# The seventh product's result is copied out of PSUM by ScalarE before VectorE adds to it

## The chip, the cores and the metric

The program runs on one core of one Trainium2 chip. The metric is the device time of one execution in microseconds. A core has five engines that matter here, each with its own in-order queue of instructions: TensorE (PE in the profile: matrix products, into the on-chip accumulator memory PSUM), VectorE (DVE), ScalarE (ACT), GpSimd (POOL), and SyncE (SP), which issues most of the transfers between the chip's main memory and the on-chip memory SBUF. An instruction starts when its own engine has reached it and when the semaphores on which it waits have been raised by other engines. A late instruction delays all that stand behind it in its queue.

## The reference, cut to what matters

The model has two layers over 1024 latent tokens of width 1024. The change lies in the second (odd) layer, the multi-scale pooling mixer, in its input projection:

```python
z = h @ p["w_in"]                       # 1024 tokens x 1024  @  1024 x 4096
u, g = jnp.split(z, [W_POOL], axis=-1)  # values u and gates g, 2048 wide each
d = multiscale_pool(u.reshape(bn * rows, GRID_W, W_POOL))   # window means minus u, per 64-token row
y = jnp.einsum("bngi,gij->bngj", d, p["w_grp"]).reshape(bn, n, W_POOL) * p["scale"]
return (y * jax.nn.silu(g)) @ p["w_out"]
```

The kernel folds `w_grp` into the value half of `w_in` beforehand (the tiles `wfold`), so the values come out of one product and only have to be pooled, scaled and multiplied by silu of the gates.

## The kernel before, in words

Everything is laid out with channels on the 128 partitions and tokens along the free axis. The input `h` of the second layer is held as 8 channel tiles of 1024 tokens. The value product and the gate product of two output tiles (2 x 128 channels, 1024 tokens) make one **block**; there are eight blocks (`m` = 0, 2, ... 14), each with a value product and then a gate product.

Each of these products is done by a Strassen-like scheme in the function `quad`: the 2 x 2 arrangement of output quarters (two channel tiles `i`, two token halves `h`) is made from seven products in place of eight. Every one of the seven is 12 matmuls: 4 channel steps times 3, because fp32 accuracy is made from a high and a low part of both operands (high x high, high x low, low x high; lines L989, L991, L992). So a block is 2 x 7 x 12 = 168 matmuls of 128x128 by 512. The weights of the seven products are sums and differences made on VectorE and split into high and low parts (`wquad`; ACT casts the high part at L102, DVE subtracts to get the low part at L103); they are loaded two tiles at a time by SP into the buffers `wr_v` and `wr_g`.

The seven products of a `quad` accumulate in three PSUM banks, named `qa`, `qc` and `qb` in the profile, out of a ring of four. In the order of the program:

- product 1 into `qa`; ACT copies `qa` to `qb` (L1005), so that `qb` starts from product 1;
- product 5 into `qc`; ACT copies it to an SBUF tile as a kept part of quarter (1,1) (L1033, `s_v` or `s_g`);
- product 6 onto `qb`; ACT copies that as a kept part of quarter (0,1);
- product 2 onto `qa`: quarter (0,0) is complete and ACT takes it out;
- **product 7 onto `qb`** (operand `x_t3`): with the kept part of quarter (1,1) it makes that quarter. This is the place of the change;
- product 3 onto `qc` (operand `x_b22`): with the kept part of (0,1) it makes that quarter, taken out by VectorE's add;
- product 4 onto `qb` (operand `x_t4`): completes quarter (1,0).

Product 4 accumulates onto the same bank out of which the result of product 7 has to be read first, so PE's first matmul on `x_t4` waits until whoever reads `qb` after product 7 is done. Before the change that reader is VectorE, which adds the kept part straight out of PSUM: `vp<-qb_v,s_v` at L1470 for the values and `y<-qb_g,s_g` at L1481 for the gates. Only in the last gate product (`m == NK - 2`) ACT copies `qb` into the output tile first (L1479) and VectorE adds in SBUF.

The code emits instructions with priorities, the evacuations with a high one; a list scheduler that estimates durations then sets the order in each engine's queue. So PE's queue often holds the start of the next product between two products of this one, and the order of VectorE's queue mixes the adds with the pooling (L1372 to L1390), the weights' sums and splits, and the sums for the third matrix product (L913 to L916). A change in one instruction's engine can therefore move others.

Of the kernel before, what the change touches and what calls it, by code (L numbers as in the profile page):

```python
# [55 lines left out]
def body(ctx, tc, xT, ctxT, cc, ccol, modT, modW, win, gw, wout, wu, grp, wg, wo1, small, edge, ident, outT):  # L56
    nc = tc.nc
    mult, add, sub = ALU.mult, ALU.add, ALU.subtract
# [16 lines left out]
    def dtile(name, dt=F32):  # L75
        return dpool.tile([P, S], dt, tag="d", name=name)
# [69 lines left out]
    def col(o, n=1):  # L146
        return sm[:, o : o + n]
# [69 lines left out]
    def mod_tile(t, l, m, raw, vecs, junk):  # L217
        for i, vec in enumerate(vecs):
            nc.vector.scalar_tensor_tensor(out=junk, in0=raw, scalar=1.0, in1=vec,
                                           op0=mult, op1=mult, accum_out=t[:, i, m : m + 1])  # L220
        n = len(vecs)
        v = t[:, :n, m]
        nc.vector.tensor_tensor(out=v, in0=v, in1=col(O_MB + l * 3 * KT + m).to_broadcast([P, n]), op=add)
# [6 lines left out]
    def load_c(i, t, part=slice(0, D)):  # L230
        nc.sync.dma_start(t, cc[i, part].partition_broadcast(P))
        nc.scalar.activation(t, t, AF.Silu)
# [420 lines left out]
    with ExitStack() as actx:  # L653
# [88 lines left out]
        for j in range(KT):  # L742
# [27 lines left out]
            if state is None:  # L770
                for m in range(2 * KT, 3 * KT):
# [5 lines left out]
                    in1=col(O_MB + 2 * KT, KT), op=add)  # L777
# [173 lines left out]
    def wquad(src, name, ring, late=False):  # L951
        raw = []
        for i in range(2):
            r = wpool.tile([P, D], F32, tag="wr", name=f"wr_{name}_{i}")
            loaded[0] = nc.sync.dma_start(r, src[i])
            raw.append(r)
        a11, a12 = [raw[0][:, h] for h in HALF]
        a21, a22 = [raw[1][:, h] for h in HALF]

        def op(v, i):  # L960
            t = ring(f"wq_{name}_{i}")
            split(v, t[:, HALF[0]], t[:, HALF[1]], nc.vector)
            return t

        p1 = op(a11, 1)
        if late:
            p4 = op(a22, 4)
        s3 = ttile(f"ws_{name}")
        nc.vector.tensor_tensor(out=s3, in0=a11, in1=a21, op=sub)
        nc.vector.tensor_tensor(out=a21, in0=a21, in1=a22, op=add)  # L970
        nc.vector.tensor_tensor(out=a11, in0=a21, in1=a11, op=sub)
        if not late:
            p5 = op(a21, 5)
        p6 = op(a11, 6)
        p2 = op(a12, 2)
        p7 = op(s3, 7)
        nc.vector.tensor_tensor(out=a12, in0=a12, in1=a11, op=sub)
        if late:
            p5 = op(a21, 5)
        p3 = op(a12, 3)  # L980
        if not late:
            p4 = op(a22, 4)
        return p1, p2, p3, p4, p5, p6, p7
# [16 lines left out]
    def quad(w, name, ops, put, ahead=None):  # L1000
        p1, p2, p3, p4, p5, p6, p7 = w
        a, c, b = psum(f"qa_{name}"), psum(f"qc_{name}"), psum(f"qb_{name}")
        prod(a, p1, ops["b11"], True, False)
        with tc.high_priority(offset=EVAC):
            evac = nc.scalar.copy(b, a)  # L1005
        prod(c, p5, ops["t1"], True, False)
        with tc.high_priority(offset=EVAC):
            put(1, 1, c, 0)
        prod(b, p6, ops["t2"], False, False)
        with tc.high_priority(offset=EVAC):  # L1010
            put(0, 1, b, 0)
        prod(a, p2, ops["b21"], False, True)
        with tc.high_priority(offset=EVAC):
            put(0, 0, a, None)
        w = None
        if ahead is not None:
            with tc.issue_after(evac.ins):
                w = ahead()
        prod(b, p7, ops["t3"], False, False)
        with tc.high_priority(offset=EVAC):  # L1020
            put(1, 1, b, 1)
        prod(c, p3, ops["b22"], False, True)
        with tc.high_priority(offset=EVAC):
            put(0, 1, c, 1)
        prod(b, p4, ops["t4"], False, True)
        with tc.high_priority(offset=EVAC):
            put(1, 0, b, None)
        return w


    def keep_part(parts, name, i, x):
        parts[i] = ttile(f"s{i}_{name}")
        nc.scalar.copy(parts[i], x)  # L1033
# [275 lines left out]
    def v_weights(m, ring):  # L1309
        return wquad([wfold[(m + i) // 4][(m + i) % 4].rearrange("p k c -> p (k c)") for i in range(2)], f"v{m}", ring)  # L1310
# [42 lines left out]
    def rows(t):  # L1353
        return t.rearrange("p (r t) -> p r t", t=ROW)
# [37 lines left out]
    NK = 2 * KT  # L1392
# [12 lines left out]
    def y_keep(m):  # L1405
        b11, b12, b21, b22 = y_blocks(m)
        for name, v in (("b11", b11), ("b21", b21), ("b22", b22)):
            y_store(m, name, v)

    def y_sums(m):  # L1410
        t = block_sums(*y_blocks(m), vtile(f"yt3_{m}"), nc.vector)
        for name in ("t1", "t2", "t3", "t4"):
            y_store(m, name, t[name])
# [18 lines left out]
    def y_operands(part, raws, names=BOPS, alloc=None):  # L1432
        for name in names:
            y_operand(yops[part], part, name, next(raws),
                      alloc or (dtile if name in ("b11", "b21", "t4") else d2tile))
# [11 lines left out]
    def wo1_weights(part, m):  # L1447
        return wquad([wo1[m + i, part] for i in range(2)], f"wo{part}_{m}", wo1_ring,
                     part == 1 and m >= KT - 4)
# [3 lines left out]
    for m in range(0, NK, 2):  # L1453
        wv = wv0 if m == 0 else v_weights(m, ring_x)
        if m == 0:
            for i in range(4):
                vp = wpool.tile([P, D], F32, tag=("wh", "wl")[i % 2], name=f"vp{i}")[:, : NR * PW]
                vp = vp.rearrange("p (r t) -> p r t", t=PW)
                nc.gpsimd.memset(vp[:, :, 0:PADW], 0.0)
                nc.gpsimd.memset(vp[:, :, PADW + ROW : PW], 0.0)  # L1460
                vps.append(vp)
        parts = {}

        def to_tokens(i, h, x, part):
            if part is None:
                nc.scalar.copy(token[i][h], rows(x))
            elif part == 0:
                keep_part(parts, f"v{m}", i, x)
            else:
                nc.vector.tensor_tensor(out=token[i][h], in0=rows(x), in1=rows(parts[i]), op=add)  # L1470

        def to_gate(i, h, x, part):
            v = ys[m + i][:, HALF[h]]
            if part == 0:
                keep_part(parts, f"g{m}", i, x)
                return
            if part == 1:
                if m == NK - 2 and i == 1:
                    nc.scalar.copy(v, x)  # L1479
                    x = v  # L1480
                nc.vector.tensor_tensor(out=v, in0=x, in1=parts[i], op=add)  # L1481
                x = v
            silu[0] = nc.scalar.activation(v, x, AF.Silu)

        token = [[vps[2 * i + h][:, :, PADW : PADW + ROW] for h in range(2)] for i in range(2)]
        quad(wv, f"v{m}", bx, to_tokens)
        if m > 0:
            y_sums(m - 2)
        wq = wquad([wg[m + i] for i in range(2)], f"g{m}", ring_x)
        for i in range(2):  # L1490
            ys[m + i] = dtile(f"y{m + i}")
        if m == 0:
            cL2 = dtile("cL2")
            load_c(0, cL2)
        elif m <= KT:
            n = 2 * KT + m - 2
            for q in range(2):
                raw = dtile(f"mod1_{n + q}")
                nc.sync.dma_start(raw, modT[1, n + q])
                mod_tile(m1, 1, n + q, raw, (cL2,), raw)  # L1500
        if m == NK - 2:
            y_operands(0, iter([dtile] + [xtile] * (4 - 1)), BOPS[:4])
        for i in range(2):
            for h in range(2):
                pool(m + i, h, vps[2 * i + h])
        w = quad(wq, f"g{m}", bx, to_gate, (lambda: wo1_weights(0, 0)) if m == NK - 2 else None)
        if m == NK - 2:
            with tc.issue_after(silu[0].ins):
                y_operands(0, iter([xtile] * 7), BOPS[4:])
        for i in range(2):  # L1510
            for h in range(2):
                gt = rows(ys[m + i][:, HALF[h]])
                nc.vector.scalar_tensor_tensor(out=gt, in0=token[i][h], scalar=col(O_OS + m + i), in1=gt,  # L1513
                                               op0=mult, op1=mult)
        y_keep(m)
# [21 lines left out]
    for m in range(0, KT, 2):  # L1537
        parts = {}
# [174 lines left out]
    m = KT - 4  # L1713
# [159 lines left out]
```

## Time and profile before

| what | before |
|---|---|
| median of 3 runs | 1298.3 us (1296.32 to 1300.41) |
| the profiled execution's own time | 1293.97 us |
| its span, first to last instruction | 1292.2 us |
| PE busy | 1273.8 us (99%) |
| DVE busy | 1142.7 us (88%) |
| ACT busy | 632.4 us (49%) |
| the eight blocks of value and gate products | about 813 to 1125 us of the span |

Times in the profile's rows are microseconds from the span's start, with the duration behind; in rows of groups the mean is in nanoseconds. A bracket at a row's end is the time for which the engine stood idle just before it, and what released it. The matmuls of PE overlap in the profile: each lasts 0.39 us, but one starts every 0.23 us when nothing is waited for, so a stall is read from the starts.

### The profile page before, as it was taken

What the parts mean: (1) busy time and instruction counts of PE and PEld (TensorE: products, weight loads), DVE (VectorE), ACT (ScalarE), POOL (GpSimd) and SP (SyncE); (2) the same over time, 40 slices, a digit from 0 to 9 for tenths busy, and PEclk for the clock granted to TensorE, in tenths of its full rate; (3) what the DMA queues carried; (4) which work ended last, traced back from release to release, by engine and by line L of the source; (5) the groups of instructions that cost most, each with busy time, mean ns of one, the idle gap of its engine ahead of it and who ended that gap; (6) DMA issues with size and microseconds to landing.
All of it is one profiled execution on the core that took longest, in us unless ns stands there. A gap on an engine that the chain in (4) does not pass through costs nothing. (4 is left out here: it accounts for less than half of the span.)

```text
span 1292.2 us, 15780 instructions
## 1 busy us (share of the span) xinstructions
PE 1273.8 (99%) x5630; PEld 1025.1 (79%) x5630; DVE 1142.7 (88%) x1758; ACT 632.4 (49%) x921; POOL 353.8 (27%) x180
## 2 busy tenths in 40 slices
PE   9999999999999999999999999999999999999996
PEld 4468888888888888888887887788888888788885
DVE  6979999999999989999789757998999986987876
ACT  4343656566657633237435345734333444654543
POOL 3063655675558603543210022000000000000002
PEclk9999999999999999999999999999999999999998
DMA  9933111121112133542555356244234324768723
GB/s 371 354 120 150 58 41 66 41 74 41 66 41 90 58 108 111 184 146 88 171 190 187 130 171 204 82 155 147 86 134 131 123 101 153 256 232 280 276 80 130
DMA packets 82899, 181.80 MB, mean 141 GB/s; under 512 B 7810, under 2 KB 27650, under 8 KB 82820
## 3 DMA queue, kind: packets, MB, share of 16 engines
q1 hardware_dynamic: 74372, 176.60, 39.4%
q10 hardware_dynamic: 8448, 4.20, 1.1%
q8 instruction: 44, 0.72, 0.2%
q14 instruction: 35, 0.29, 0.1%
HBM read 136.72 MB, written 44.04 MB: 140 GB/s over the span
## 5 line engine op out<-in xcount | busy, mean ns | idle before, releaser
L501 DVE SCALAR_TENSOR_TENSOR conv<-u,sm,conv 128x505 f32<-128x505 f32 (+6 forms) x224 | 153.7, 744 | 0.9
L1674 POOL TENSOR_TENSOR o<-x,rr 128x256 f32<-128x256 f32 (+1 forms) x10 | 9.7, 996 | 441.7 <-ACT rr L1610 441.7
L501 POOL TENSOR_TENSOR l<-l,l 128x1280 f32<-128x1280 f32 (+1 forms) x23 | 64.0, 2797 | 92.0 <-DVE l L501 76.8
L501 ACT ACTIVATE l<-g,sm 128x512 f32<-128x512 f32 (+1 forms) x96 | 58.6, 619 | 57.6 <-PE g L501 55.9
L281 PE MATMUL fold<-graw,wu 128*128 128x512 f32 x128 | 57.2, 608 | 0.0
L501 PE MATMUL wob<-ybh,wh_wob 128*128 128x512 f32 x128 | 50.6, 396 | 0.0
L501 PE MATMUL gb<-h0h,wl_gb 128*128 128x512 f32 x128 | 49.9, 390 | 0.3 <-POOL wl_gb L501 0.3
L501 PE MATMUL vg<-h0h,wl_vg 128*128 128x512 f32 x128 | 50.0, 390 | 0.0
L501 PE MATMUL gb<-h0l,wh_gb 128*128 128x512 f32 x128 | 49.8, 389 | 0.0
L501 PE MATMUL gb<-h0h,wh_gb 128*128 128x512 f32 x128 | 49.8, 389 | 0.0
L501 PE MATMUL vg<-h0l,wh_vg 128*128 128x512 f32 x128 | 49.8, 389 | 0.0
L501 PE MATMUL wob<-ybh,wl_wob 128*128 128x512 f32 x128 | 49.8, 389 | 0.0
L501 PE MATMUL vg<-h0h,wh_vg 128*128 128x512 f32 x128 | 49.8, 389 | 0.0
L501 PE MATMUL va<-h0h,wh_va 128*128 128x512 f32 x128 | 49.8, 389 | 0.0
L501 PE MATMUL va<-h0l,wh_va 128*128 128x512 f32 x128 | 49.8, 389 | 0.0
L501 PE MATMUL va<-h0h,wl_va 128*128 128x512 f32 x128 | 49.8, 389 | 0.0
L501 PE MATMUL wob<-ybl,wh_wob 128*128 128x512 f32 x128 | 49.8, 389 | 0.0
L501 DVE TENSOR_TENSOR_SCAN l<-l,l 128x256 f32<-128x256 f32 (+1 forms) x32 | 48.7, 1521 | 1.1
L102 ACT CAST wq_g<-wr_g 128x512 fp32r<-128x512 f32 x48 | 28.2, 620 | 42.9 <-DMA wr_g<-wg 14.0
L281 PEld LDWEIGHTS fold<-graw,wu 128*128 128x128 f32 x128 | 24.9, 196 | 30.4 <-issue 29.6
L103 POOL TENSOR_TENSOR wl_wu<-wr_wu,wh_wu 128x1024 fp32r<-128x1024 f32 x8 | 19.2, 2399 | 108.1 <-ACT wh_wu L102 108.1
L501 POOL TENSOR_TENSOR l<-l,uc 128x1280 f32<-128x1280 f32 x16 | 48.2, 3034 | 0.0
(611 smaller groups left out, 4329.1 us busy)
## 6 DMA issues: line engine op xcount, KB each, us to landing
mod<-modT SPq DMA_DIRECT2D x20, 512.0 KB, 5.1
x_part<-xp SPq DMA_DIRECT2D x32, 256.0 KB, 2.8
mod<-modT SPq DMA_DIRECT2D x32, 256.0 KB, 3.1
wr_v<-wfold SPq DMA_DIRECT2D x16, 512.0 KB, 3.6
wr_g<-wg SPq DMA_DIRECT2D x16, 512.0 KB, 4.6
wr_wo<-wo SPq DMA_DIRECT2D x16, 512.0 KB, 5.3
y_b<-y SPq DMA_DIRECT2D x24, 256.0 KB, 3.7
y_t<-y SPq DMA_DIRECT2D x24, 256.0 KB, 4.1
```

Of the source, the lines that this page charges most:

```text
L102: return (nc.scalar.copy(hi, src), eng.tensor_tensor(out=lo, in0=src, in1=hi.bitcast(F32), op=sub))
L103: eng.tensor_tensor(out=lo, in0=src, in1=hi.bitcast(F32), op=sub))
L281: nc.tensor.matmul(ps, w[:, kc], gs[i], start=(i == 0), stop=(i == 3))
L501: last[eng] = f(*args, **kw)
L1674: nc.gpsimd.tensor_tensor(out=outs[k // per][:, k % per], in0=x1[k][:, cols], in1=rr, op=mult)
```

## The change

After product 7 of every value product and of every gate product, ACT copies `qb` out of PSUM into the SBUF tile that will hold the result, and VectorE adds the kept part in place, both operands in SBUF. The last gate product did so already.

```diff
         def to_tokens(i, h, x, part):
             if part is None:
                 nc.scalar.copy(token[i][h], rows(x))
             elif part == 0:
                 keep_part(parts, f"v{m}", i, x)
             else:
-                nc.vector.tensor_tensor(out=token[i][h], in0=rows(x), in1=rows(parts[i]), op=add)
+                x = rows(x)
+                if i == 1:
+                    nc.scalar.copy(token[i][h], x)
+                    x = token[i][h]
+                nc.vector.tensor_tensor(out=token[i][h], in0=x, in1=rows(parts[i]), op=add)
 
         def to_gate(i, h, x, part):
             v = ys[m + i][:, HALF[h]]
...
             if part == 1:
-                if m == NK - 2 and i == 1:
+                if i == 1:
                     nc.scalar.copy(v, x)
                     x = v
                 nc.vector.tensor_tensor(out=v, in0=x, in1=parts[i], op=add)
```

ACT's queue grows from 938 rows to 953, by 8 copies at the new L1472 and 7 more at what is now L1483; PE's, VectorE's and SP's queues keep their number of rows, but not their order within the eight blocks.

ACT's queue in the value product of the third block, before the change (`wq_g` are casts of the gate weights that follow, `vp` the tiles of values, `qa_v` and `qb_v` the PSUM banks):

```order
L1466 COPY vp_6543<-qa_v_7157 128x8x64
L102 CAST wq_g_6_7276<-wr_g_0_7262 128x512
L102 CAST wq_g_2_7279<-wr_g_0_7262 128x512
L102 CAST wq_g_7_7282<-ws_g_7269 128x512
L102 CAST wq_g_3_7286<-wr_g_0_7262 128x512
L102 CAST wq_g_4_7289<-wr_g_1_7264 128x512
L1005 COPY qb_g_7348<-qa_g_7346 128x512
```

And the same place with the change:

```order
L1466 COPY vp_6543<-qa_v_7161 128x8x64
L102 CAST wq_g_6_7281<-wr_g_0_7267 128x512
L102 CAST wq_g_2_7284<-wr_g_0_7267 128x512
L102 CAST wq_g_7_7287<-ws_g_7274 128x512
L1472 COPY vp_6552<-qb_v_7163 128x8x64
L102 CAST wq_g_3_7291<-wr_g_0_7267 128x512
L102 CAST wq_g_4_7294<-wr_g_1_7269 128x512
L1005 COPY qb_g_7353<-qa_g_7351 128x512
```

The copy out of `qb_v` stands behind the cast of `wq_g_7` and ahead of the casts of `wq_g_3` and `wq_g_4`, which wait for a subtraction on VectorE (L977).

VectorE's queue at the same place, before the change:

```order
L103 TENSOR_TENSOR wq_g_7_7282<-ws_g_7269,wq_g_7_7282 128x512
L977 TENSOR_TENSOR wr_g_0_7262<-wr_g_0_7262 128x512
L1372 TENSOR_TENSOR ws_0_4_7306<-ws_0_2_7304 128x8x73
L1470 TENSOR_TENSOR vp_6552<-qb_v_7159,s_v_7185 128x8x64
L1470 TENSOR_TENSOR vp_6546<-qc_v_7158,s_v_7199 128x8x64
L103 TENSOR_TENSOR wq_g_3_7286<-wr_g_0_7262,wq_g_3_7286 128x512
```

And with the change:

```order
L103 TENSOR_TENSOR wq_g_7_7287<-ws_g_7274,wq_g_7_7287 128x512
L1372 TENSOR_TENSOR ws_0_4_7311<-ws_0_2_7309 128x8x73
L977 TENSOR_TENSOR wr_g_0_7267<-wr_g_0_7267 128x512
L1372 TENSOR_TENSOR ws_0_8_7313<-ws_0_4_7311 128x8x65
L1474 TENSOR_TENSOR vp_6546<-qc_v_7162,s_v_7203 128x8x64
L1474 TENSOR_TENSOR vp_6552<-vp_6552,s_v_7189 128x8x64
L1381 TENSOR_TENSOR ws_0_8_7313<-ws_0_8_7313,eg 128x8x8
L103 TENSOR_TENSOR wq_g_3_7291<-wr_g_0_7267,wq_g_3_7291 128x512
```

The add on `vp_6552` no longer reads `qb_v`; it has moved behind the add out of `qc_v`, and one pooling step (L1372) and L977 have changed places, and a further L1372 now stands ahead of both adds.

ACT's queue in the value product of the second block, before:

```order
L102 CAST wq_g_1_6958<-wr_g_0_6954 128x512
L1466 COPY vp_6543<-qa_v_6849 128x8x64
L102 CAST wq_g_5_6965<-wr_g_1_6956 128x512
L102 CAST wq_g_6_6968<-wr_g_0_6954 128x512
L102 CAST wq_g_2_6971<-wr_g_0_6954 128x512
L102 CAST wq_g_7_6974<-ws_g_6961 128x512
L1005 COPY qb_g_7024<-qa_g_7022 128x512
```

And with the change:

```order
L102 CAST wq_g_1_6961<-wr_g_0_6957 128x512
L1466 COPY vp_6543<-qa_v_6851 128x8x64
L102 CAST wq_g_5_6968<-wr_g_1_6959 128x512
L1472 COPY vp_6552<-qb_v_6853 128x8x64
L102 CAST wq_g_6_6971<-wr_g_0_6957 128x512
L102 CAST wq_g_2_6974<-wr_g_0_6957 128x512
L102 CAST wq_g_7_6977<-ws_g_6964 128x512
```

Here the copy stands directly behind the cast of `wq_g_5`, which waits for a sum on VectorE (L970).

## The prediction

> **What bounds the kernel now.** First the page's busy times, then the busy time by stretches: the eight blocks, and all that follows them.
>
> ```profile
> span 1292.2 us, 15780 instructions
> PE 1273.8 (99%) x5630; PEld 1025.1 (79%) x5630; DVE 1142.7 (88%) x1758; ACT 632.4 (49%) x921; POOL 353.8 (27%) x180
> ...
> 813.00:1125.00 312.00, 309.27 (x1358) 254.16 (x1357) 283.22 (x490) 136.69 (x234) 0.95 (x8) 1.00 0.39 133
> 1125.00:1292.20 167.20, 156.11 (x729) 129.55 (x727) 129.64 (x197) 80.77 (x133) 9.65 (x10) 0.98 0.59 205
> ```
>
> In the blocks PE is busy 309.27 of 312 us at full granted clock (1.00), VectorE 283.22 (91%), ScalarE 136.69 (44%). So PE bounds this stage, and nothing that is done for VectorE can be worth more than PE's idle time, 312 - 309.27 = 2.7 us by this count. The change adds and removes no matmul. The next question is which waits make up that idle time; this is the view of PE's waits in the same stretch (total, times, longest):
>
> ```profile
> PE qb_g L989 <- ACT y L1479: 0.8, 1, 0.8
> PE qb_v L989 <- DVE vp L1470: 0.7, 2, 0.5
> PE qc_v L989 <- ACT s_v L1033: 0.7, 1, 0.7
> PE qb_v L989 <- ACT qb_v L1005: 0.6, 1, 0.6
> ```
>
> Five stalls in all. Two of them are the wait that the change touches: product 4 of a value product waits for VectorE's add out of `qb`. Two (L1005 and L1033, both in the first block) and the one for L1479 (in the last block) are waits for ScalarE, which the change leaves. The fifteen places changed are eight value and seven gate products, and PE stalled at two of them. The first of these, in the third block, in the timeline:
>
> ```profile
> 906.49 0.61 ACT L102 CAST wq_g<-ws_g 128x512 fp32r<-128x512 f32 x1
> ...
> 907.35 0.39 PE L992 MATMUL qb_v<-x_t3h,wq_v 128*128 128x512 f32 x1
> ...
> 909.72 0.76 DVE L1372 TENSOR_TENSOR ws<-ws 128x584 f32<-128x584 f32 x1
> ...
> 910.29 0.39 PE L991 MATMUL qa_g<-x_b11l,wq_g 128*128 128x512 f32 x1
> 910.40 0.68 DVE L1470 TENSOR_TENSOR vp<-qb_v,s_v 128x512 f32<-128x512 f32 x1
> 910.52 0.39 PE L992 MATMUL qa_g<-x_b11h,wq_g 128*128 128x512 f32 x1
> ...
> 911.13 0.50 PE L989 MATMUL qb_v<-x_t4h,wq_v 128*128 128x512 f32 x1 [0.22 <-DVE vp L1470]
> 911.47 0.39 PE L991 MATMUL qb_v<-x_t4l,wq_v 128*128 128x512 f32 x1
> ```
>
> Product 7's last matmul ends at 907.35 + 0.39 = 907.74. VectorE comes to the add only at 910.40, because other work stands ahead in its queue, the pooling step at 909.72 last. PE's pace is 910.52 - 910.29 = 0.23 us; the next start comes 0.61 us later, and the one after it 0.34. So the stall costs 0.38 + 0.11 = 0.49 us. The same place in the fourth block:
>
> ```profile
> 949.13 0.39 PE L992 MATMUL qa_g<-x_b11h,wq_g 128*128 128x512 f32 x1
> 949.26 0.68 DVE L1470 TENSOR_TENSOR vp<-qb_v,s_v 128x512 f32<-128x512 f32 x1
> ...
> 949.99 0.50 PE L989 MATMUL qb_v<-x_t4h,wq_v 128*128 128x512 f32 x1 [0.47 <-DVE vp L1470]
> ...
> 950.33 0.40 PE L991 MATMUL qb_v<-x_t4l,wq_v 128*128 128x512 f32 x1
> ```
>
> Starts 0.86 and 0.34 us apart: 0.63 + 0.11 = 0.74 us.
>
> **The change, part by part.** The groups of instructions by shape give the prices (count, busy, mean ns, idle before):
>
> ```profile
> L1470 DVE TENSOR_TENSOR vp<-qb_v,s_v 128x512 f32<-128x512 f32 x8 | 5.5, 682 | 0.0
> L1481 DVE TENSOR_TENSOR y<-qb_g,s_g 128x512 f32<-128x512 f32 x7 | 4.8, 682 | 2.4 <-PE qb_g L992 2.4
> L1481 DVE TENSOR_TENSOR y<-y,s_g 128x512 f32<-128x512 f32 x1 | 0.7, 687 | 0.0
> L1466 ACT COPY vp<-qb_v 128x512 f32<-128x512 f32 x8 | 4.7, 586 | 8.7 <-PE qb_v L992 8.6
> L1479 ACT COPY y<-qb_g 128x512 f32<-128x512 f32 x1 | 0.6, 572 | 0.0
> ```
>
> *VectorE's adds.* Fifteen adds out of PSUM at 682 ns become fifteen in SBUF; the one of that kind that exists took 687 ns. So VectorE's work changes by 15 x 5 ns = 0.1 us, and VectorE is not PE's bound: 0 us of the span, hidden under PE's matmuls. Without that cover it would be +0.1.
>
> [...]
>
> *ScalarE's copies.* Fifteen at 572 to 586 ns: 8.6 to 8.8 us more, so ACT goes from 136.7 to about 145.4 of 312 us. That lies under PE's matmuls as long as no copy comes late. If the cover were gone at every place, the price is 8.7 us and what ACT waits for ahead of it.
>
> *The two stalls.* In the third block the last cast ahead of the new copy in ACT's queue ran from 906.49 to 907.10, before product 7 had ended (907.74). So the copy can begin at about 907.8 and end at 908.4, where VectorE's add ended at 911.08; PE wants the bank at 910.52 + 0.23 = 910.75. The cover is 2.3 us. The order of the fourth block is the same, four weight casts and then the copy. So both stalls go: -0.49 - 0.74 = -1.23 us.
>
> *The new wait at the thirteen other places.* Behind the copy on ACT stand casts of weights and the copy of the next `qa` (L1005); a late copy delays these by 0.6 us, and casts are awaited by VectorE's splits. The two tightest places, by ACT's queue with the change held against the trace, are the second block's products. Value, then gate:
>
> ```profile
> 869.72 0.39 PE L992 MATMUL qb_v<-x_t3h,wq_v 128*128 128x512 f32 x1
> ...
> 870.32 0.62 ACT L102 CAST wq_g<-wr_g 128x512 fp32r<-128x512 f32 x1 [4.11 <-DVE wr_g L970]
> ...
> 872.67 0.39 PE L989 MATMUL qb_v<-x_t4h,wq_v 128*128 128x512 f32 x1
> ...
> 889.16 0.62 ACT L102 CAST wq_v<-ws_v 128x512 fp32r<-128x512 f32 x1
> ...
> 890.41 0.68 DVE L1481 TENSOR_TENSOR y<-qb_g,s_g 128x512 f32<-128x512 f32 x1
> ...
> 891.71 0.39 PE L989 MATMUL qb_g<-x_t4h,wq_g 128*128 128x512 f32 x1
> ```
>
> In the value product the copy stands behind the cast that waited 4.11 us for a sum on VectorE and ended at 870.94; with 0.59 us for the copy the bank is free at 871.53, and PE wants it at 872.67: 1.1 us of cover. In the gate product the cast ends at 889.78, the copy at 890.37, PE wants the bank at 891.71: 1.3 us, more than VectorE left it (891.09). I take 0 for all thirteen. The bounds: below, nothing can be gained where PE didn't stall; above, one such wait for ACT has a price in this trace, in the last block's gate product, where the copy is already there:
>
> ```profile
> 1119.85 1.05 ACT L102 CAST y_b21h<-yr_b 128x1024 fp32r<-128x1024 f32 x1 [0.22 <-DMA yr_b<-y_b]
> ...
> 1121.30 0.39 PE L992 MATMUL qa_wo<-y_b11h,wq_wo 128*128 128x512 f32 x1
> ...
> 1121.81 0.57 ACT L1479 COPY y<-qb_g 128x512 f32<-128x512 f32 x1
> ...
> 1122.44 0.50 PE L989 MATMUL qb_g<-x_t4h,wq_g 128*128 128x512 f32 x1 [0.76 <-ACT y L1479]
> 1122.77 0.39 PE L991 MATMUL qb_g<-x_t4l,wq_g 128*128 128x512 f32 x1
> ```
>
> Starts 1.14 and 0.33 us apart: 0.91 + 0.10 = 1.0 us. There the casts ahead of the copy wait for transfers; at the thirteen places they wait for VectorE or for nothing. Two of the thirteen going that way is as far as I would stretch it: +2.0.
>
> *The moved orders.* The scheduler also moves a few of VectorE's instructions by one to seven places, and SP issues the third block's gate weights a little earlier against the stores of results. The cover for weights is that the casts wait for the loads while PE doesn't: no wait of PE on weights appears in the view above. 0 us, with +-0.5 for a place that I can't see.
>
> *Does the gain reach the end?* The chain of waits, in order of time, at the later stall and at the end of the blocks:
>
> ```profile
> 949.34 0.61 DVE vp L1470
> 949.99 0.50 PE qb_v L989
> ...
> 1105.14 0.24 PE qb_v L992
> 1105.39 5.39 DMA yr_t<-y_t
> ```
>
> From 949.99 to 1105.14 the chain is PE's matmuls; then a load that a PE matmul released. So when PE comes earlier, the loads and casts at the last block's stall come earlier too, and the gain is not eaten there. The end of the kernel is unchanged.
>
> The sum: -1.23 + 0 + 0 + 0 = -1.2 us. On the profiled execution (span 1292.2, its own time 1293.97, so 1.8 us around the span) that makes a span of 1291.0 and a time of 1292.7. That execution was 4.3 us quicker than the median of the three runs shown; against the median, 1298.3 - 1.2 = **1297.1 us**. About 0.3% (3.9 us) is what a measurement of this kernel can tell from no change, so I call it the same.
>
> **The rivals.**
>
> *Given back.* The stalls go, but PE, 1.2 us earlier, waits as much longer at 1122.44 because the transfers there don't follow PE. For it: the casts ahead of that copy waited for `yr_b`, and the DMA queues are shared. Against it: the chain above. Time 1298.3; no change as well.
>
> *Slower: copies behind casts.* ACT's queue is in order. Where the cast ahead waits for VectorE (L970 in the second block), a late VectorE now holds up PE by way of ACT, also where its add was not needed. It decides from the point at which the cast ends more than 1.1 us later than in this trace. Priced at 1.0 us each, seven places make 7.0 - 1.2 = +5.8: 1304.1; all fifteen +13.8: 1312.1. For it: ACT's waits on L970 and on weights are long (4.11 us above). Against it: PE's margin at the two tightest places. [...]
>
> *Faster than can be put down to two stalls.* All five stalls go and the reordered queues leave none. With the first block's two priced like the last block's, at 1.0 us, that is 1.23 + 3 x 1.0 = 4.2 us: 1294.1. Against it: ACT's waits of the first and last block are not touched.
>
> *That it doesn't do what it says.* The order shows all fifteen copies; what could fail is that VectorE's add was not the reason of the two stalls, then 1298.3, as in the first rival.
>
> **How the numbers follow.** Forecast 0.62; given back, or the wrong reason, 0.22; slower, from five late copies on (5.0 - 1.2 = 3.8 us), 0.08; faster by all stalls 0.08. The first two are no change by the 0.3%, so: faster 0.08, same 0.84, slower 0.08. The range: at the lower end 0.5 us for the moved orders, half of the fastest rival's further 3.0 us and the runs' half spread of 2.0 (1296.32 to 1300.41) make 1297.1 - 4.0 = 1293.1; at the upper end the two late copies (+2.0) and the same half spread and 0.5 make 1301.6.
>
> **What would show it.** Right: in PE's waits no row `qb_v L989 <- DVE vp` (now L1474), none on the new L1472 or on the gate copies but the last; the add in place at 680 to 690 ns, the copies at 570 to 590; PE idle in the blocks 1.5 us rather than 2.7. Wrong: a wait of `qb_v` or `qb_g` on ACT in the second block, or on weights (L102, L103) anywhere; the stall at the last block's copy longer than 1.0 us by what was won before; PE starts further apart than 0.23 us where nothing is waited for.

## The result, and the profile after

The changed kernel took 1292.55 us, the median of 7 executions (1289.92 to 1298.68); beside it the kernel before took 1299.33 us, also of 7 (1296.32 to 1302.02). The ratio is 0.9958, with a 95% interval of 0.9938 to 0.9979. Two later comparisons gave 0.9976 (0.9960 to 0.9991) and 0.9948 (0.9932 to 0.9963), and the medians were 6.8, 3.9 and 6.1 us apart. So the kernel is faster, by 4 to 7 us where 1.2 us were forecast, and the time lies 0.55 us below the lower end of the range; the two later medians, 1295.56 and 1293.81 us, lie inside it. The prediction called its 1.2 us no change, because it took 0.3% as the least that can be told from none. Measured, the change is 0.24 to 0.52%, and none of the three intervals holds 1.

The profiled execution of the changed kernel took 1297.47 us, 4.9 us more than its median, and that of the kernel before 1293.97 us, 5.4 us less than its median. Put beside each other, these two profiles show a loss of 3.5 us. The page's busy times of the changed kernel, and its busy times in the stretch of the eight blocks (length, then PE, weight loads, VectorE, ScalarE, GpSimd, granted clock, DMA share, GB/s):

```profile
span 1295.7 us, 15787 instructions
PE 1274.6 (98%) x5630; PEld 1025.1 (79%) x5630; DVE 1143.5 (88%) x1758; ACT 637.3 (49%) x936; POOL 354.7 (27%) x180
```

```profile
813.00:1125.00 312.00, 309.30 (x1359) 254.34 (x1359) 282.81 (x491) 141.88 (x249) 0.95 (x8) 1.00 0.39 132
```

ScalarE has 15 instructions more in the stretch (249 for 234) and 5.2 us more of busy time; PE is idle for 2.7 us, as before. What PE waits for, though, has changed (total, times, longest):

```profile
PE qb_g L989 <- ACT y L1483: 0.9, 1, 0.9
PE qc_v L989 <- ACT s_v L1033: 0.7, 1, 0.7
PE qb_v L989 <- ACT qb_v L1005: 0.6, 1, 0.6
PE qc_g L989 <- DVE vp L1474: 0.5, 1, 0.5
```

The three waits for ScalarE are the ones of before. The wait of `qb_v` for VectorE is gone, and there is one in `qc_g` that the kernel before did not show. The groups of the touched instructions (count, busy, mean ns, idle before):

```profile
L1474 DVE TENSOR_TENSOR vp<-vp,s_v 128x512 f32<-128x512 f32 x8 | 5.4, 680 | 0.0
L1485 DVE TENSOR_TENSOR y<-y,s_g 128x512 f32<-128x512 f32 x8 | 5.4, 680 | 0.0
...
L1472 ACT COPY vp<-qb_v 128x512 f32<-128x512 f32 x8 | 4.7, 581 | 1.0 <-PE qb_v L992 1.0
L1483 ACT COPY y<-qb_g 128x512 f32<-128x512 f32 x8 | 4.7, 583 | 6.7 <-PE qb_g L992 6.7
```

The prices are those of the prediction. A copy costs 581 to 583 ns, and an add with both operands in SBUF 680 ns, where it took 682 ns from PSUM. Only ScalarE's total was forecast too high: 15 x 0.58 = 8.7 us were expected in the blocks, and its busy time there rose by 5.2 us. Rows of instructions that follow each other without a pause overlap in the profile (two casts of 0.62 us make one row of 1.14 us), and the busy time counts the overlap once. So the prices are not where the 4 to 7 us come from.

### The profile page after: what moved, and what is told of

It is laid out like the page before. It is cut to its first block, busy times and chain, and to the rows that moved or that the text cites. A ratio compares the mean times of both kernels' runs of the same rounds, so it can differ in the third digit from the quotient of the medians.

```text
span 1295.7 us, 15787 instructions
## 1 busy us (share of the span) xinstructions
PE 1274.6 (98%) x5630; PEld 1025.1 (79%) x5630; DVE 1143.5 (88%) x1758; ACT 637.3 (49%) x936; POOL 354.7 (27%) x180
## 4 chain that ended last, share of the span: by engine, by line
PE 76%; DMA 10%; DVE 8%; ACT 3%; issue 2%; POOL 1%; SPq 0%; POOLq 0%; DVEq 0%; ACTq 0%
PE vg L501 7%; PE wob L501 7%; PE va L501 7%; PE gb L501 7%; PE xb L501 6%; PE g L501 4%; PE fold L281 3%; PE ga L135 2%; PE ga L501 2%; PE ga L134 2%; PE ga L133 2%; PE xbc L501 2%; DMA x_part<-xp 1%; DMA wr_wo<-wo 1%; DMA mod<-modT 1%
## 5 line engine op out<-in xcount | busy, mean ns | idle before, releaser
L103 POOL TENSOR_TENSOR wl_wu<-wr_wu,wh_wu 128x1024 fp32r<-128x1024 f32 x8 | 19.2, 2395 | 108.7 <-ACT wh_wu L102 108.1
L102 ACT CAST wq_v<-wr_v 128x512 fp32r<-128x512 f32 x48 | 28.2, 619 | 41.9 <-DMA wr_v<-wfold 16.5
```

What stands on the lines that cost most here:

```text
L102: return (nc.scalar.copy(hi, src), eng.tensor_tensor(out=lo, in0=src, in1=hi.bitcast(F32), op=sub))
L103: eng.tensor_tensor(out=lo, in0=src, in1=hi.bitcast(F32), op=sub))
```

## The experiments

**Both kernels once more.** The first two runs are the two kernels themselves, with many executions and a second profile of each, since the first two profiles each came from an end of its kernel's spread.

> The kernel before, unchanged, timed against itself: it shows how far two sets of executions of one program lie apart, and gives a second profile of it. All theories expect a ratio of 1.000; by the scatter of the seven runs before (1296.32 to 1302.02) within 0.998 to 1.002. Theory A (the gain is PE's stalls inside the eight blocks) expects the two waits of qb_v L989 on VectorE's L1470 again, 0.5 and 0.7 us. Theory C (the executions differ by how late transfers land behind the blocks, whichever the kernel) expects the stretch from the last gate product's stall to the end to differ from the first profile by 2 to 6 us while the blocks keep their length within 0.5.

> The changed kernel, unchanged. Measured so far: ratio 0.9958 (0.9938 to 0.9979), with a profiled execution at 1297.47 us that has new stalls of 3 us behind the blocks, where five of seven runs lie at 1289.9 to 1292.6. Theory A (two stalls of 1.23 us in the blocks): ratio 0.999. Theory B (the gain lies behind the blocks, in the order that the scheduler made new there): ratio 0.996 again, and in a quick execution the stretch behind the blocks 3 us or more shorter than in the first profile of the change. Theory C (executions scatter): nearer to 1 than 0.9958.

The kernel before took 1299.48 us (12 executions, ratio to its other runs 1.0003, 0.9989 to 1.0016), the changed one 1295.56 us (12, ratio 0.9976). PE's waits in the second profile of the kernel before, behind the first block:

```profile
PE qb_v L989 <- DVE vp L1470: 2.3, 2, 1.9
PE qb_wo L989 <- ACT s_wo L1033: 1.2, 1, 1.2
PE qb_g L989 <- ACT y L1479: 0.9, 1, 0.9
PE qb_g L989 <- DVE y L1481: 0.2, 1, 0.2
PE qb_wo L989 <- ACT b_wo L1534: 0.2, 1, 0.2
```

The wait that the change removes, 0.7 us in the first profile, is 2.3 us here, 1.9 of it at one place, and a gate product waits for VectorE too (L1481). By the starts of the matmuls a stall in the prediction's profile cost 0.27 us more than the idle time in its bracket (0.22 and 0.49, 0.47 and 0.74); with that, the three stalls here cost 2.5 + 3 x 0.27 = 3.3 us. A fourth, at the sixth block's value product, has too little idle time for this view; by the starts it costs 0.3 us more. Why VectorE was late in the third block can be read in the timeline:

```profile
899.07 1.23 DVE L219 SCALAR_TENSOR_TENSOR mod<-mod,cL 128x1024 f32<-128x1024 f32 x1 [1.62 <-DMA mod<-modT]
...
902.14 0.69 DVE L103 TENSOR_TENSOR wq_g<-wr_g,wq_g 128x512 fp32r<-128x512 f32 x1 [1.64 <-ACT wq_g L102]
903.53 0.69 DVE L969 TENSOR_TENSOR ws_g<-wr_g,wr_g 128x512 f32<-128x512 f32 x1 [0.70 <-DMA wr_g<-wg]
...
905.43 0.69 DVE L916 TENSOR_TENSOR y<-y,y 128x512 f32<-128x512 f32 x1 [0.48 <-DMA y_b<-y]
...
911.77 0.68 DVE L1470 TENSOR_TENSOR vp<-qb_v,s_v 128x512 f32<-128x512 f32 x1
912.50 0.50 PE L989 MATMUL qb_v<-x_t4h,wq_v 128*128 128x512 f32 x1 [1.87 <-DVE vp L1470]
```

VectorE stood idle for 1.62 + 1.64 + 0.70 + 0.48 = 4.4 us on its way, three times for a transfer and once for a cast, which had itself waited 3.8 us for a transfer. Then it worked through its queue without a pause from 905.43 to the add at 911.77, and PE stood from 910.63 on. The four waits depend on when transfers land, which would make this stall differ from execution to execution; between the two profiles of the kernel before it did, 0.2 and 1.9 us.

**The same, only where the stalls were.** If the two stalls are all that the change is worth, two copies do what fifteen do.

```diff
+                x = rows(x)
+                if i == 1 and m in (4, 6):
+                    nc.scalar.copy(token[i][h], x)
+                    x = token[i][h]
```

> The copy on ScalarE only in the value products of the third and fourth block, the two places where PE stalled; the instruction orders of all engines behind the blocks stay as before. Theory A: all of the change's gain, -1.2 us (ratio 0.9991), and no wait of qb_v on VectorE at the two places. Theory B: no more than these 1.2 us, so well short of 0.9958. If the ratio is 0.996 or less, theory B falls.

1298.62 us, ratio 0.9998 (0.9985 to 1.0011): no gain that can be told from nothing. The interval still holds the 0.9991 that 1.2 us would make, but not the 0.9976 of the whole change, which was measured beside it. PE's waits for VectorE in this kernel:

```profile
PE qb_g L989 <- DVE y L1485: 1.7, 3, 0.8
PE qb_v L989 <- DVE vp L1474: 0.5, 1, 0.5
```

The two stalls are gone from their places (the value products of the third and fourth block) and others have come: three gate products, and a value product of a later block, together 2.2 + 4 x 0.27 = 3.3 us, as much as the first three in the unchanged kernel's second profile. VectorE's add in the third block's gate product began 3.3 us after product 7 had ended there, where in both profiles of the kernel before it began after 1.2 us. So VectorE stays behind, and PE meets that lateness at the next bank which only VectorE can release.

**The moved order alone.** With a copy in the last block's value product only, the scheduler moves instructions behind the blocks nearly as the whole change does, and the blocks keep their adds out of PSUM.

```diff
+                if i == 1 and m == NK - 2:
```

> The copy on ScalarE only in the value product of the last block: PE's two stalls in the blocks stay, but the queues of VectorE, ScalarE, PE and SP behind the blocks get nearly the order that the whole change gives them (the same rows of SP and PE differ there). Theory A: ratio 1.000, as the stalls stay. Theory B: most of the gain, ratio 0.996 to 0.997, with both stalls of 0.5 and 0.7 us still there. Theory C: 1.000 within the scatter.

1298.38 us, ratio 0.9989 (0.9973 to 1.0006), which can't be told from nothing. PE waited 2.5 us at two value products. So the moved order is not shown to be worth anything.

**Values without gates.** All eight value copies, no gate copy but the one that was there:

```diff
+                if i == 1:
+                    nc.scalar.copy(token[i][h], x)
+                    x = token[i][h]
...
                 if m == NK - 2 and i == 1:
```

> The copy on ScalarE in all eight value products, none of the seven gate products. Theory D (transfers land late in most executions, VectorE falls behind in the third to sixth block, and PE then waits at the next place at which VectorE's add has to release the bank; the change wins by taking VectorE out of all these places) expects part of the gain: with only blocks 3 and 4 changed, PE's waits moved to the gate products there (1.1, 0.5 and 0.9 us) and to a value product (0.8); here the value products' can't, so waits of qb_g on L1485 of 1 to 2 us in all are left, ratio 0.998 to 0.9995. Theory A in its first form (only the two places count, 1.2 us) expects 0.999 and no waits at gate products. Theory B (order behind the blocks, which is nearly that of the whole change) expects the whole change's 0.9967.

1295.72 us, ratio 0.9961 (0.9946 to 0.9977). PE still waited for VectorE, at two gate products:

```profile
PE qb_g L989 <- DVE y L1485: 0.8, 2, 0.6
```

Beside the runs above that was as good as the whole change (0.9976). The two were therefore run again, side by side:

> The changed kernel a third time. So far 0.9958 (0.9938 to 0.9979) and 0.9976 (0.9960 to 0.9991) to the kernel before; its two profiled executions were among its slower ones (1297.5 and 1298.9 us) and had waits of 1.1 to 1.5 us behind the blocks (weights of the next product, copies b_wo). Theory D (PE no longer waits for VectorE in the blocks, 3 us less there; transfers behind the blocks give back 1.5 to 3 us in some executions): ratio 0.996 to 0.998; blocks 311 to 312 us from the first value matmul to the last gate product, against 314 to 315 in the typical execution of before; a quick execution has no waits of over 1 us behind the blocks.

> The copy in the eight value products only, a second time and beside the whole change. First time: 0.9961 (0.9946 to 0.9977) from six runs. If the gate copies win their 1 to 1.3 us of waits as well, the whole change is 0.001 quicker than this; if they are worth nothing or cost something by way of the moved orders behind the blocks (139.6 us there against 141.8 and 143.3 with the whole change), this one is as quick or quicker: 0.996 to 0.997.

The whole change took 1293.81 us (1292.04 to 1295.3; ratio 0.9948, 0.9932 to 0.9963), the values alone 1297.74 us (1293.91 to 1300.48; ratio 0.9976, 0.9963 to 0.9989). The two intervals just touch; here the gate copies were worth 3.9 us, in the comparison before it nothing. The value copies are thus shown to matter. For the gate copies the profiles speak (two waits in either profile of the values alone, none in this one of the whole change), but the times do not settle their size. The gate copies by themselves were not run.

This profile of the whole change lies near its median (1293.59 us), and so does the second of the kernel before (1297.76 us, with a median of 1299.48). They are the pair to compare. Blocks two to six, first the kernel before, then the whole change:

```profile
858.00:1048.00 190.00, 187.48 (x823) 153.71 (x822) 176.15 (x316) 73.33 (x130) 0.00 (x0) 1.00 0.36 121
```

```profile
858.00:1048.00 190.00, 190.00 (x840) 157.34 (x839) 177.87 (x319) 77.95 (x142) 0.00 (x0) 1.00 0.36 123
```

With the change PE has no idle time at all in 190 us and starts 17 matmuls more. The fifth block's value product shows how:

```profile
984.44 0.39 PE L992 MATMUL qb_v<-x_t3h,wq_v 128*128 128x512 f32 x1
984.87 0.58 ACT L1472 COPY vp<-qb_v 128x512 f32<-128x512 f32 x1
...
987.84 0.39 PE L989 MATMUL qb_v<-x_t4h,wq_v 128*128 128x512 f32 x1
...
989.99 0.68 DVE L1474 TENSOR_TENSOR vp<-vp,s_v 128x512 f32<-128x512 f32 x1
```

ScalarE began right behind product 7 (984.44 + 0.39 = 984.83) and had copied the bank by 985.45. PE wrote to the bank again at 987.84, without a wait. VectorE came to the add only at 989.99, 5.2 us after product 7; the latest of these adds in the kernel before, the one of 1.87 us of stall above, came after 4.3 us. VectorE is as late as ever or later, and at this place it holds nobody up.

From the start of the first matmul of the blocks to the start of the last on `qb_g`, the kernel before needs 314.7 us (813.09 to 1127.75) and the changed one 309.5 us (814.34 to 1123.84): 5.2 us less. Of that, 3.6 us are the four stalls above, and 1.0 us is the wait at the last block's copy, which cost 0.9 + 0.27 = 1.2 us there and by the starts 0.2 us here.

**VectorE made later.** If VectorE's lateness is the cost, more work in its queue should cost the kernel before more than the changed one. Ahead of each add of a seventh product's kept part, an added maximum of that part with itself, 16 x 0.68 = 10.9 us in all:

```diff
+                if i == 1:
+                    nc.vector.tensor_tensor(out=parts[i], in0=parts[i], in1=parts[i], op=ALU.max)
```

> The kernel before, with one more VectorE operation of 128x512 (0.68 us, the maximum of the kept part with itself, which changes no value) ahead of each add of a seventh product's result: 16 x 0.68 = 10.9 us more VectorE work in the blocks, where VectorE was 280 of 312 us busy. Theory D: VectorE falls behind further, PE's waits of qb_v and qb_g on the adds grow; slower than before by 2 to 8 us (ratio 1.0015 to 1.006). If VectorE's lateness isn't what PE waits for, 1.000.

> The changed kernel with the same 16 extra operations on VectorE. Theory D: PE no longer waits for VectorE's add after product 7, so the extra work is hidden until VectorE is late with something else (weights, or the bank of qc): at most 2 us slower than the changed kernel, ratio 0.997 to 0.9985 to the kernel before, and well below the kernel before with the extra work. If the change only moved the wait, it loses as much as the kernel before does, and the two ratios differ by no more than the 0.003 that the change is worth.

Both expectations fell. The kernel before became 1.2 us slower, which the interval can't tell from nothing (1302.25 us beside 1301.03; ratio 1.0008, 0.9994 to 1.0021). The changed kernel, with a ratio of 0.9948 to 0.9976 otherwise, was left at 1.0000 (0.9985 to 1.0015): 3 to 7 us. So the amount of VectorE's work does not by itself foretell what PE loses. The first of the two runs is no clean test, though: the longer VectorE queue made the scheduler move PE's queue too. In its profile the fifth block's product 4 starts 8.9 us after product 7 has ended in the value product and 5.3 us in the gate product, with PE at work on other products in between; in the kernel before it is 3.0 and 2.8 us. That gives VectorE more time. For the changed kernel the profile shows one reason. ScalarE and PE in the fifth block's value product:

```profile
985.73 0.62 ACT L102 CAST wq_g<-ws_g 128x512 fp32r<-128x512 f32 x1
988.57 0.74 DVE L1521 SCALAR_TENSOR_TENSOR y<-vp,sm,y 128x512 f32<-128x512 f32 x1
989.40 0.59 ACT L1472 COPY vp<-qb_v 128x512 f32<-128x512 f32 x1 [3.05 <-DVE y L1521]
990.04 0.50 PE L989 MATMUL qb_v<-x_t4h,wq_v 128*128 128x512 f32 x1 [1.65 <-ACT vp L1472]
```

The copy waited 3.05 us for VectorE, not behind a cast but for an instruction that reads a `vp` tile (L1521), and PE waited 1.65 us for the copy. Product 7's last matmul started at 984.8, so it had ended by 985.2. The release of the bank needs two things with the change, ScalarE and a free result tile, and the second is VectorE's to give. This stall explains 1.65 + 0.27 = 1.9 us of the 3 to 7. In this profile the stretch behind the blocks is longer as well, 145.2 us where the changed kernel has 141.3 to 143.3; the next run's profile shows the same 145.2 us without the extra work, so I can't assign that part.

**The last gate product.** There ScalarE's copy is the one PE waits for. In the changed kernel, that one add goes back to reading PSUM:

```diff
-                if i == 1:
+                if i == 1 and m < NK - 2:
```

> The changed kernel, but in the last gate product VectorE adds straight out of PSUM and ScalarE doesn't copy. In all profiles so far PE waits there 1.0 to 2.0 us for ScalarE's copy, whose queue holds casts that wait for transfers. Theory: VectorE's queue at that place is as long or longer (it makes the low parts of the same operands), so no gain, ratio to the kernel before 0.996 to 0.999. If ScalarE's queue there is the whole price, 1 us better than the changed kernel.

1298.28 us, ratio 0.9980 (0.9964 to 0.9997), against 0.9976 with the copy: no better. At that place PE now waits for VectorE:

```profile
PE qb_g L989 <- DVE y L1485: 1.5, 1, 1.5
```

**VectorE given room.** The last pair leaves out the eight modulation vectors of the second layer (its output gates are then 1) that are computed beside blocks two to five: their loads and VectorE's instructions at L219 and L223. In blocks two to six that takes some 10 us of VectorE's work away:

```profile
L219 DVE SCALAR_TENSOR_TENSOR mod<-mod,cL 128x1024 f32<-128x1024 f32 x7 | 8.5, 1219 | 1.8 <-DMA mod<-modT 1.6
L223 DVE TENSOR_TENSOR m<-m,sm 128x1 f32<-128x1 f32 x7 | 1.1, 152 | 0.0
```

```diff
+            nc.vector.memset(m1[:, 0, 2 * KT : 3 * KT], 1.0)
-        elif m <= KT:
+        elif False:
```

> The kernel before without the eight modulation vectors that blocks 2 to 5 compute beside the products (their 512 KB loads and two VectorE operations of 1.2 us each a block are left out, so the gates of the output are set to 1). Theory D: VectorE, 33 to 36 of 38 us busy in blocks 2 to 6 and 29.6 in block 7, where PE never waits for it, gets 2.9 us a block of room, so PE's waits of qb_v and qb_g on its adds vanish: blocks 311 to 312 us long, ratio 0.9965 to 0.998. If the waits came from elsewhere, 1.000.

> The changed kernel with the same work left out. Theory D: in the blocks there is no wait on VectorE left that the room could remove, so it gains little over the changed kernel (0 to 1 us), and it is no quicker than the kernel before without that work by more than 1 us (the change has lost its reason): ratio 0.996 to 0.998. If the change's gain had another source than VectorE's lateness, it stays 3 us ahead of the kernel before without the work.

Without that work the kernel before took 1293.74 us (ratio 0.9953, 0.9937 to 0.9969) and the changed one 1295.12 us (0.9961, 0.9945 to 0.9977). Blocks two to six of the kernel before without it, and of the changed one:

```profile
858.00:1048.00 190.00, 190.00 (x840) 157.39 (x839) 173.96 (x301) 73.64 (x132) 0.00 (x0) 1.00 0.31 108
```

```profile
858.00:1048.00 190.00, 190.00 (x839) 157.36 (x839) 173.23 (x299) 78.58 (x141) 0.00 (x0) 1.00 0.32 111
```

PE has no idle time in either. In the third to sixth value product of the kernel before, the add now begins 0.3 to 0.6 us after product 7 has ended, where it began after 2.1 to 4.3 us in the second profile; PE wants the bank after 3.0. With VectorE on time the adds straight out of PSUM hold nobody up. The room is worth 6.2 us to the kernel before and nothing to the changed one (1293.81 us with the work), the change wins nothing more (the intervals overlap), and the kernel before comes to the time that the change gave it. So what the change wins in the blocks is PE's waits for a late VectorE. These two kernels take away both VectorE's work and its transfers of 512 KB each. That 10.9 us of added work cost the kernel before only 1.2 us may mean that the transfers, and what VectorE waits for, weigh more than the work, but that run's order had moved too. A kernel with the loads but without the arithmetic was not run, so this stays open.

No kernel run here was measurably quicker than the changed one.

## Why the prediction was wrong in size and right in kind

- **"So both stalls go: -1.23 us."** This is the step that failed. Both stalls did go, by the mechanism named, but they were mis-sized, because the whole sum came from one execution. That execution, at 1293.97 us, was quicker than every other execution of this kernel in the study (the next was 1294.81). The prediction knew that it was 4.3 us quicker than the median and yet took its stalls as the stalls of all executions. In the second profile the same term is 3.6 us. The upper bound that the prediction set, "nothing that is done for VectorE can be worth more than PE's idle time", 2.7 us, was a bound for that execution alone. It was also too low there: idle time leaves out the 0.27 us by which a stall costs more than its bracket, and the prediction's own prices for its five stalls add up to 4.2 us.
- **Stalls tied to places.** The prediction took "below, nothing can be gained where PE didn't stall" and set thirteen places to nothing. With copies only at the two places where PE had stalled, 3.3 us of stalls stood at four other places and no gain could be measured. Without the thirteen the two bring little or nothing, because the thirteen are where the lateness goes.
- **The costs** held. Copies were forecast at 572 to 586 ns and took 581 to 583; adds were forecast to stay near 687 ns and took 680. Out of PSUM they had taken 682 in the kernel before, 2 ns more. ScalarE's busy time was over-forecast (5.2 us for 8.7), which cost nothing.
- **The new wait at the thirteen other places, 0 us**, held: in three profiles of the changed kernel PE waits for no copy but the last block's. It was closer than the 1.1 us of cover that the prediction gave the tightest place: in the first profile the fourth block's copy, behind casts that had waited for VectorE, ended at 949.40, and PE wrote to the bank at 949.56. The rival "slower" needed a late VectorE ahead of the copy; it came only with 10.9 us of extra work, and by way of the result tile rather than of a cast.
- **The moved orders, 0 +- 0.5 us.** One of three profiles has a stall here, in the fourth block. The add out of `qc_v` now stands ahead of the add in place, and still it is late:

```profile
952.26 0.68 DVE L1474 TENSOR_TENSOR vp<-qc_v,s_v 128x512 f32<-128x512 f32 x1
953.00 0.50 PE L989 MATMUL qc_g<-x_t1h,wq_g 128*128 128x512 f32 x1 [0.54 <-DVE vp L1474]
```

  With 0.27 for the restart it costs 0.8 us. The bank `qc` is still VectorE's to release, and there the change does not help. I read this stall as VectorE's lateness met at the next bank rather than as a price of the new order, which puts this add earlier; no run separates the two.
- **"Does the gain reach the end?"** It does, within what the profiles can tell. The wait at the last block's copy was 0.8 and 0.9 us in the kernel before, and 0.9, 1.7 and none in the changed one. In one of three it is longer by 0.8 us, of 1.2 forecast to be won, which was one of the prediction's signs of being wrong. So the rival "given back" is not ruled out for single executions; the medians show that it does not take the whole gain. Behind the blocks, up to the first matmul of `qc_l`, the kernel before took 140.4 and 141.5 us and the changed one 143.3, 141.8 and 141.3. The long one is the first profile of the changed kernel, with waits of PE there for a split and for casts:

```profile
PE qb_wo L989 <- ACT b_wo L1538: 1.5, 2, 1.1
PE qc_wo L992 <- DVE wq_wo L103: 1.0, 1, 1.0
```

  The wait for a split (L103) is one of the prediction's signs of being wrong. It stands in the first two profiles of the changed kernel (1.0 and 0.9 us), in neither of the kernel before, and not in the third of the changed one; the kernel before with extra VectorE work has it too (1.1 us). So it isn't tied to the change alone, and about 1 us given back behind the blocks stays possible. Waits for ScalarE there are in both kernels (1.2 us for `s_wo` above). What makes them long or short wasn't settled.
- **The rival "faster"**, 1294.1 us, came nearest in time, but not by its mechanism: the first block's two waits for ScalarE stayed (0.7 and 0.6 us in the first profile after), and the gain lay in waits that the profile it was argued from did not show.
- **"PE idle in blocks 1.5 us rather than 2.7"** failed in the first profile after (2.7 us) and would have misled by itself. The 1.5 was also mixed from two measures: of 2.7 us of idle time, the two stalls' brackets (0.22 + 0.47) can take only 0.7; the row that was right was the missing wait of `qb_v` for VectorE.

What is not accounted for: in the blocks the stalls at VectorE's adds explain 0.4 to 3.6 us (1.2 and 3.6 in the two profiles before, less the 0 to 0.8 left with the change) of the 3.9 to 6.8 between the medians. The first block is no part of the rest, for PE's two waits there are 0.6 and 0.7 us in all fourteen profiles. What remains lies at the last block's copy, in the stretch behind the blocks (139.6 to 145.2 us over the fourteen profiles) and in the stretch ahead of them, after which the blocks' first matmul starts between 811.6 and 817.5 us. These differ between executions by as much as what is missing (the blocks began at 814.2 to 817.5 us in the changed kernel alone), and the profiles don't tell which of them the medians hold.

## What to carry to other kernels

A profile is one execution: before a stall of half a microsecond is priced, set the profile's own time against the median, and where they differ by more than the effect looked for, take the stall's size from further profiles or give it a bound from the difference. A stall that comes from a late engine belongs to that engine's lateness, not to the place where it shows; mending the place alone moves it to the next buffer that the engine must release (here 3.3 us of stalls at four other places, with copies at two). An extra copy that lets another engine release a PSUM bank can pay although it makes no instruction cheaper (here 4 to 7 us, with adds of 680 ns for 682), so long as the copy waits neither for the late engine nor for a tile that this engine still reads.

## What had not been expected of the hardware

In the kernel before with VectorE's extra work, PE ran at half pace after one stall:

```profile
916.00 0.50 PE L989 MATMUL qb_v<-x_t4h,wq_v 128*128 128x512 f32 x1 [1.91 <-DVE vp L1472]
...
918.40 0.63 PE L992 MATMUL qb_v<-x_t4h,wq_v 128*128 128x512 f32 x1
918.83 0.63 PE L989 MATMUL qb_v<-x_t4h,wq_v 128*128 128x512 f32 x1
```

PE stood still for 1.91 us. Some 1.4 us after it had begun again, matmuls started 0.43 us apart instead of 0.23, for 3.4 us. Eight matmuls so cost 8 x 0.20 = 1.6 us more, which takes the price of the stall from 2.2 to 3.8 us. A stall of 1.87 us in the unchanged kernel, quoted above, had no such stretch. So less than 2 us of standing still was followed by the half pace once and not another time.

The granted clock shows the stretch too, and its changes keep to a step. From its first record to its fall to 0.50 at the end, the first profile of the kernel before has 1269.76 us and that of the changed kernel 1273.17 us, 372 and 373 times 3.4133 us. In the kernel with extra work the clock fell to 0.50 at 787.7 and at 917.4 us, 38 such steps apart. So I laid windows of that length through the span, in the unchanged kernel's second profile from the fall at its end (1287.95 us, 110 steps behind 912.51). These are the window with the stall and the one behind it, in the kernel with extra work and then in the unchanged one (PE's busy time follows the length; the clock is the third number from the end):

```profile
914.00:917.41 3.41, 1.50 (x7) 1.19 (x7) 3.38 (x8) 1.40 (x3) 0.00 (x0) 1.00 0.00 0
917.41:920.83 3.42, 3.42 (x10) 2.67 (x9) 3.39 (x8) 0.79 (x2) 0.00 (x0) 0.50 0.11 19
```

```profile
909.10:912.51 3.41, 1.54 (x8) 0.94 (x6) 3.41 (x7) 1.22 (x3) 0.00 (x0) 1.00 0.00 0
912.51:915.92 3.41, 3.41 (x15) 2.83 (x16) 3.41 (x8) 0.75 (x2) 0.00 (x0) 1.00 0.34 112
```

PE was idle for 1.91 us of the one window and for 1.87 us of the other. From 20 to 1275 us of the spans, the fourteen profiles show the clock at 0.50 at five places, for 3.4 to 3.5 us each. Two are in this kernel; PE had been idle for 3.10 us between 781.70 and 787.96 ahead of the first. One each is in the second profile of the changed kernel (2.92 us between the same times), in the second of the values alone (a stall of 2.09 us) and in that of the last gate product on VectorE (2.04 us between 1161.30 and 1167.90). Idle time of that length also went free: between 781.70 and 787.96, 2.57 us in the first profile of the values alone, 2.54 us in the kernel with copies at two places and 2.30 us in the first profile of the changed kernel left the clock at 1.00. The last of these is one stall, from 783.72 to 786.01, and it lies across two windows, 0.67 us in the one and 1.62 us in the next. So a window didn't have to be idle throughout: 1.91 us of 3.41 was followed by half the clock, 1.87 us was not. That the place of a stall in the windows decides fits these cases and is my reading of them; no run moved a stall to try it.
